# Sixteen places for x, divided mixer steps with a planner margin, and GpSimd's low parts in two instructions

## The chip, the cores and the metric

The kernel runs on one core of one Trainium2 chip. The metric is the device time of one execution in microseconds, taken as the median of several runs. Five engines work in parallel, each through its own list of instructions in order: TensorE (PE; its weight loads are PEld), VectorE (DVE), ScalarE (ACT), GpSimd (POOL) and SyncE (SP), which here issues nearly all transfers from memory.

## What is computed

The input x is 512 positions of 2048 values. Two blocks follow one another. The first has two layers, the second has one layer with two branches side by side:

```python
# first block
for i in range(2):
    h = rmsnorm(x, norm_g[i])
    p = h @ (fox_w_in if i == 0 else swa_w_in)     # q, k, v, gate
    y = fox_attention(...) if i == 0 else swa_attention(...)
    x = x + (y * silu(gate)) @ w_out
x = rmsnorm(x, final_g)
# second block, the mixer
proj = x @ w_in
rw, hg = token_shift(proj[..., :RWKV_COLS]), proj[..., RWKV_COLS:]
o_rwkv = rwkv7_branch(rw, ...)     # 16 heads of 64: S = S*w + (S a) b + v k ; o = S r, group norm
o_hgrn = hgrn2_branch(hg, ...)     # 8 heads of 128: gated linear attention in chunks of 64
y = concat(o_rwkv, o_hgrn) @ w_out
out = layer_norm(ALPHA * x + y)
```

Everything is float32, and the large products are made in three terms so that they keep its accuracy.

## The kernel before

**Tiling.** A weight chunk is a tile `raw` of 128 x 512 (256 KB), loaded by SyncE into one of three buffers. ScalarE copies it in a shorter format into `wh`, GpSimd makes the low part `wl` = `raw` - `wh` in one instruction, and TensorE adds three products for each k-tile of 128: high x high, low x high, high x low (`proj<-hh,wh`, `proj<-hl,wh`, `proj<-hh,wl`). One chunk serves four k-tiles, so twelve matmuls. The activations of a layer are kept in 16 pairs `hh`, `hl`, each made by a *feed* from one k-tile of x (ScalarE makes `hh`, VectorE makes `hl`, and VectorE adds up `rsb` for the norm).

**Order.** `stream` goes over the slots (block of outputs, k-tile) of all weight products and writes them into TensorE's list. Everything else, called side work, is cut into steps that stand in threads: attention heads, the eight RWKV units (`rwkv_unit`, u = 0 to 7, two heads each), the HGRN units. Between two slots `side` takes the steps that are ready. What is ready is decided when the program is built, by a planner: `Clock` keeps a time for each engine, `Engine.cost` gives each instruction's cost, and `ready` compares a step's inputs with TensorE's planned time. `MARGIN` adds 0.1 us to each result and `BUDGET` lets 1.8 us of side work in at a time:

```python
    def ready(self, th):
        return th["steps"] and th["ready"] <= self.clk and all(
            self.ev.get(e, 1e9) <= self.clk for e in th["steps"][0][1]) and self.banks(
                th["steps"][0][0]) <= self.clk
```

A step's instructions on all engines enter the lists together. An engine that comes to one whose input isn't there stands still, with all that is behind it in its list.

**The start.** `start` loads the first tiles of x and the first chunks; eight places for x are in use (tags `t`, `pt`, `yf`, `sg`, two each), and x tile n + 8 is loaded after feed n. The SyncE queue is in order, so chunks behind such a load wait too.

**An RWKV unit.** Its prepare steps (p_kk, p_dec, p_ops and others) make decays and operands, `lev` steps invert a triangular matrix for each of the four chunks of the sequence (VectorE's `invt`, `ly`, `x`; TensorE's small products `t<-td,yh`, `t<-wd,ly`, `t<-ly,wd` of 16 to 32 rows), `ch_z`, `ch_u`, `ch_s` and `ch_o` run the state through the chunks (`chz`, `chu`, `sbd`, `y`), and f_1, f_2, f_3 make the group norm on `zo` with the small sums `gn`; f_3 lets TensorE transpose `zo`. All instructions are recorded by one helper, so every row of the profile has line L182 (L184 after the change).

Of the kernel before, what the change touches and what calls it, by code (L numbers as in the profile page):

```python
# [17 lines left out]
KT = 16  # L18
# [91 lines left out]
class Engine:  # L110
# [15 lines left out]
    def cost(self, m, out, ins, k):  # L126
# [80 lines left out]

class Kern:
    NRAW, NW, LEAD, LEAD_RAW, BUDGET, MARGIN, POOL_LO = 3, 3, 2, 2, 1.8, 0.1, True
# [60 lines left out]
    def split_to(self, end):  # L270
        nc = self.nc
        while self.n_split < min(end, len(self.chunks)):
# [14 lines left out]
            eng = nc.vector if self.n_split in self.extra else nc.gpsimd  # L287
            eng.tensor_tensor(out=lo, in0=t, in1=hi.bitcast(F32), op=ALU.subtract)
# [61 lines left out]
    def ready(self, th):  # L350
        return th["steps"] and th["ready"] <= self.clk and all(
# [3 lines left out]
    def banks(self, f):  # L355

        name = [n for n in f.__qualname__.split(".") if n not in ("<locals>", "f")][-1]
        t = 0.0
        for i, p in enumerate(BANKS.get(name, "")):
# [226 lines left out]
    def start(self):  # L586
# [21 lines left out]
        self.on_slot = on_slot  # L608
        self.load_raw(1)
        load_x(0)  # L610
        self.par = const("par")
        load_x(1)
# [6 lines left out]
        load_x(2)  # L619
        load_x(3)  # L620
        self.load_raw(3)
        for n in range(4, 8):
            load_x(n)
        self.split_to(1)
        feed(0)
        feed(1)
        self.split_to(2)
        feed(2)
        feed(3)

# [671 lines left out]
    def rwkv_unit(self, st, u):  # L1302
# [58 lines left out]
        def p_kk2():  # L1361
# [4 lines left out]
            self.rsqrt(m, rn)  # L1366

        def p_kk3():
            m, rn = S["m"][:, 0:512], S["rn"][:, 0:512]
            self.newton_rsqrt(rn, m, S["sq"])  # L1370
            nc.gpsimd.tensor_tensor(out=S["kq"], in0=S["kq"], in1=rn, op=ALU.mult)

        def p_dec():
# [4 lines left out]
            S["em"] = em = P("em", (128, 2, 4), bufs=3)  # L1378
            nc.scalar.activation(em[:, 0, :], cs[:, :, 64], AF.Exp, scale=-KAPPA)
            mid = P("mid", (128, 4))  # L1380
# [5 lines left out]
        def p_dec2():  # L1386
            cs = S["cs"]
            S["P"], S["Pi"] = P("pr", (128, 4, 129)), P("pt", (128, 4, 128))
# [18 lines left out]
        def p_ops4():  # L1407
            k, r = st["k", u], st["r", u]
            nc.vector.scalar_tensor_tensor(out=r, in0=r, scalar=c2["rk"], in1=k, op0=ALU.mult,
                                           op1=ALU.mult)  # L1410
            S["rh"] = P("pq", dt=F32R)
            nc.scalar.activation(S["rh"], r, AF.Copy)
# [281 lines left out]
        def f_1():  # L1694
# [6 lines left out]
            nc.scalar.activation(S["zo"][:, :, 0, :], of, AF.Square)  # L1701
# [18 lines left out]
        def seq(*items):  # L1720
            r = []
            for f, need, ev, *back in items:
# [12 lines left out]
                   (p_kk2, (), None),  # L1735
                   (p_kk3, (), None),
                   (p_dec, (), None),
# [38 lines left out]
        B = seq((p_ops4, [("mar", u)], "ops"),  # L1776
# [50 lines left out]
    def hgrn_unit(self, st, u):  # L1827
# [17 lines left out]
        def prep2():  # L1845
# [6 lines left out]

            nc.scalar.activation(t2, ls, AF.Abs, bias=c2["bma"])
# [13 lines left out]
        def prep4():  # L1867
# [6 lines left out]
                                    op=ALU.subtract)  # L1874
            nc.scalar.activation(S["d"], S["d"], AF.Exp)
# [167 lines left out]
        def seq(*items):  # L2043
            r = []
            for f, need, ev, *back in items:
# [7 lines left out]
                 (prep2, (), None),  # L2053
                 (prep3, (), None),
                 (prep4, (), None))
# [321 lines left out]
```

## Time and profile before

| | |
|---|---|
| median of three runs | 2966.38 us (2964.68 to 2971.58) |
| profiled execution | 2970.38 us, span 2968.6 us |
| mean granted clock of TensorE | 0.988 of full speed |
| TensorE, VectorE, ScalarE, GpSimd busy | 98%, 51%, 42%, 45% of the span |
| weight chunks split on GpSimd | 847 |

The stages follow in time: fox layer to about 1060 us, window layer to about 1710, RWKV to about 2400, HGRN to about 2800, then the last projection and the layer norm. A busy time counts an instruction's execution; idle time of TensorE is what the waits list explains, and a granted clock below 1 means that TensorE worked at its lower level (1.2 GHz instead of 2.4) for part of the stretch.

### The profile page before, as it was taken

Reading aid. Unit: us, or ns where it says so; the run is one execution under the profiler, and the core shown is the slowest. Engines: PE = TensorE matmul, PEld = TensorE weight load, DVE = VectorE, ACT = ScalarE, POOL = GpSimd, SP = SyncE. Lnnn points to the kernel's source line nnn. Section 1 sums busy time; section 2 is a strip of 40 time slices with the busy share of each in tenths; the row PEclk is TensorE's granted clock in tenths of the full one; section 3 lists DMA queues with packets and bytes.
Section 4 is the critical chain, followed back from the end, with each engine's and each line's share of the span. In section 5 each row is a group of like instructions: output and inputs, shape, how many; then the busy total and the mean of one; then the engine's idle time right before and its main releaser. Section 6 shows DMA issues by size and latency. Waiting matters only on the chain.

```text
span 2968.6 us, 47847 instructions
## 1 busy us (share of the span) xinstructions
PE 2911.0 (98%) x18032; PEld 2351.3 (79%) x18032; DVE 1519.0 (51%) x3374; ACT 1257.6 (42%) x2464; POOL 1332.5 (45%) x1093
## 2 busy tenths in 40 slices
PE   8999999999999999999999999999999999999997
PEld 5888888888888888888888887777777778877786
DVE  6434334343432135555541167777877566666536
ACT  6444444444433344444443354343433345445334
POOL 3444444444436544444446654333333254444583
PEclk9999999999999999999999999999999899999998
DMA  4322232332324432222234423222222222222333
GB/s 141 108 89 91 91 93 93 92 94 88 92 89 160 150 95 77 80 77 78 80 103 150 131 91 90 59 74 70 67 63 75 67 70 72 83 76 77 99 121 121
DMA packets 192087, 275.79 MB, mean 93 GB/s; under 512 B 50576, under 2 KB 65872, under 8 KB 191856
## 3 DMA queue, kind: packets, MB, share of 16 engines
q1 hardware_dynamic: 191856, 272.73, 30.4%
q8 instruction: 142, 2.33, 0.3%
q14 instruction: 89, 0.73, 0.1%
HBM read 254.51 MB, written 18.16 MB: 92 GB/s over the span
## 4 chain that ended last, share of the span: by engine, by line
PE 89%; DVE 5%; issue 2%; POOL 1%; ACT 1%; DMA 0%; SPq 0%; ACTq 0%; POOLq 0%; DVEq 0%
PE proj L182 73%; PE t L182 7%; PE s L182 6%; PE y L182 3%; DVE invt L182 1%; POOL wl L182 1%; DVE hh L182 1%; DVE gn L182 1%; DVE ly L182 1%; DVE zo L182 0%; DMA raw<-in_w_mixo_dram 0%; DVE hn L182 0%; DVE ek L182 0%; DVE raw L182 0%; DVE ez L182 0%
## 5 line engine op out<-in xcount | busy, mean ns | idle before, releaser
L182 POOL TENSOR_TENSOR wl<-raw,wh 128x512 fp32r<-128x512 f32 x847 | 1124.0, 1329 | 1567.3 <-ACT wh L182 1510.1
L182 PE MATMUL proj<-hh,wh 128*128 128x512 f32 x2624 | 1070.1, 408 | 10.8 <-ACT hh L182 6.4
L182 PE MATMUL proj<-hh,wl 128*128 128x512 f32 x2624 | 1034.2, 394 | 3.5 <-POOL wl L182 3.4
L182 PE MATMUL proj<-hl,wh 128*128 128x512 f32 x2624 | 1033.1, 394 | 3.3 <-DVE hl L182 3.1
L182 ACT ACTIVATE wh<-raw 128x512 fp32r<-128x512 f32 x848 | 531.3, 628 | 819.4 <-PE proj L182 588.5
L182 PEld LDWEIGHTS proj<-hh,wh 128*128 128x128 f32 x2624 | 497.2, 189 | 117.1 <-ACT hh L182 7.1
L182 PEld LDWEIGHTS proj<-hh,wl 128*128 128x128 f32 x2624 | 497.1, 189 | 114.9 <-POOL wl L182 7.0
L182 PEld LDWEIGHTS proj<-hl,wh 128*128 128x128 f32 x2624 | 498.4, 190 | 96.0 <-DVE hl L182 6.5
L182 PE MATMUL proj<-yh,wh 128*128 128x512 f32 (+1 forms) x632 | 246.9, 391 | 0.0
L182 PE MATMUL proj<-yh,wl 128*128 128x512 f32 (+1 forms) x632 | 245.6, 389 | 0.3
L182 ACT ACTIVATE t<-t,sm 128x257 f32<-128x257 f32 (+5 forms) x256 | 133.1, 521 | 265.6 <-DVE sm L182 203.7
L182 PE MATMUL proj<-yl,wh 128*128 128x512 f32 (+1 forms) x640 | 242.3, 387 | 0.0
L182 PEld LDWEIGHTS proj<-yh,wl 128*128 128x128 f32 x632 | 118.6, 188 | 26.1 <-POOL wl L182 1.6
L182 PEld LDWEIGHTS proj<-yl,wh 128*128 128x128 f32 x640 | 119.9, 188 | 23.8 <-issue 0.2
L182 PEld LDWEIGHTS proj<-yh,wh 128*128 128x128 f32 x632 | 118.7, 188 | 24.4 <-issue 0.6
L182 DVE TENSOR_TENSOR pt<-proj,t 128x512 f32<-128x512 f32 x32 | 22.1, 691 | 226.3 <-PE proj L182 221.7
L182 DVE TENSOR_SCALAR t<-t,sm 128x256 f32<-128x256 f32 (+3 forms) x256 | 113.5, 475 | 5.6
L182 DVE TENSOR_TENSOR qf<-proj,rsb 128x512 f32<-128x512 f32 x48 | 33.1, 691 | 161.8 <-PE proj L182 161.5
L182 DVE COPY pt<-t 128x384 f32<-128x384 f32 (+1 forms) x80 | 48.5, 607 | 81.6 <-PE t L182 81.6
L182 DVE CUSTOM_DVE_ANT_0 t<-s,c 128x128 f32<-128x128 f32 (+2 forms) x128 | 47.1, 387 | 80.1 <-PE s L182 77.8
L182 PEld LDWEIGHTS t<-ident,t 128*128 128x128 f32 x544 | 69.0, 140 | 21.0
L182 PE MATMUL t<-ident,t 128*128 128x128 f32 x544 | 85.2, 272 | 0.0
(410 smaller groups left out, 3592.4 us busy)
## 6 DMA issues: line engine op xcount, KB each, us to landing
raw<-in_w_mix_dram SPq DMA_DIRECT2D x260, 256.0 KB, 3.0
raw<-in_w_fox_dram SPq DMA_DIRECT2D x256, 256.0 KB, 3.0
raw<-in_w_swa_dram SPq DMA_DIRECT2D x144, 256.0 KB, 3.0
raw<-in_w_foxo_dram SPq DMA_DIRECT2D x64, 256.0 KB, 3.1
raw<-in_w_swao_dram SPq DMA_DIRECT2D x64, 256.0 KB, 3.1
raw<-in_w_mixo_dram SPq DMA_DIRECT2D x64, 256.0 KB, 3.2
c<-cd SPq DMA_DIRECT2D x32, 256.0 KB, 3.7
xd<-pt SPq DMA_DIRECT2D x32, 256.0 KB, 2.4
```

What stands on the lines that cost most here:

```text
L182: r = f(*a, **k)
```

## The change

Four things change. `start` gives each of the 16 tiles of x a place of its own, loads them in an order fixed at the start (par, chunks and groups of x in turn), and feeds run one further ahead. `split_to` makes `wl` on GpSimd in two instructions of 128 x 256. The planner gets other costs (GpSimd's elementwise; 0.25 us more for VectorE operations with two wide inputs and deep, short patterns), a slack for three kinds of steps, and a limit `BACKLOG`: a thread that isn't urgent waits while VectorE's or ScalarE's planned time is over 4 us ahead of TensorE's. And steps that ended in a hand-over to another engine are divided there: p_kk2, p_kk3, p_dec, p_ops4, f_1, and prep2 and prep4 of HGRN; p_kk3 and f_1 stand for them in the diff.

```diff
--- before.py
+++ after.py
@@ -145,11 +145,13 @@
-            return 0.075 + n / (1920.0 if one else 960.0) + 0.06 * bool(points) + 2 * acc
+
+            deep = 0.25 * (len(wide) > 1 and len(out.ap) > 3 and out.ap[-1][1] < 16)
+            return 0.075 + n / (1920.0 if one else 960.0) + 0.06 * bool(points) + 2 * acc + deep
...
-            return max(0.1, 0.00264 * n - 0.11)
+            return max(0.1, 0.00254 * n - 0.05)
...
+SLACK = dict(f_3=1.5, fin3=1.5, ch_z=0.4)
...
-    NRAW, NW, LEAD, LEAD_RAW, BUDGET, MARGIN, POOL_LO = 3, 3, 2, 2, 1.8, 0.1, True
+    NRAW, NW, LEAD, LEAD_RAW, BUDGET, MARGIN = 3, 3, 2, 2, 1.8, 0.1
+
+    BACKLOG = 4.0
...
             nc.scalar.activation(hi, t, AF.Copy)
-            eng = nc.vector if self.n_split in self.extra else nc.gpsimd
-            eng.tensor_tensor(out=lo, in0=t, in1=hi.bitcast(F32), op=ALU.subtract)
+
+            eng, parts = (nc.vector, 1) if self.n_split in self.extra else (nc.gpsimd, 2)
+            for i in range(parts):
+                c = slice(512 // parts * i, 512 // parts * (i + 1))
+                eng.tensor_tensor(out=lo[:, c], in0=t[:, c], in1=hi[:, c].bitcast(F32),
+                                  op=ALU.subtract)
...
     def ready(self, th):
-        return th["steps"] and th["ready"] <= self.clk and all(
+        late = 0.0 if th["first"] else max(
+            self.clock.t["vector"], self.clock.t["scalar"]) - self.BACKLOG
+        f = th["steps"][0][0] if th["steps"] else None
+        return f and max(th["ready"] + SLACK.get(step_name(f), 0.0), late) <= self.clk and all(
             self.ev.get(e, 1e9) <= self.clk for e in th["steps"][0][1]) and self.banks(
                 th["steps"][0][0]) <= self.clk
...
-        def load_x(n):
-            tag, b = (("t", 3), ("pt", 4), ("yf", 2), ("sg", 2))[n % 4]
-            xs.append(self.tmp(tag, bufs=b))
-            nc.sync.dma_start(xs[n], I["x"][n])
+        place = [(t, b) for t, b in (("t", 3), ("pt", 4), ("yf", 2), ("sg", 2), ("vf", 1), ("qf", 1),
+                                     ("vt", 2), ("q0", 1), ("q1", 1)) for _ in range(b)]
+
+        def load_x(end):
+            while len(xs) < end:
+                tag, b = place[len(xs)]
+                xs.append(self.tmp(tag, bufs=b))
+                nc.sync.dma_start(xs[-1], I["x"][len(xs) - 1])
 
         def feed(n):
             self.feed_hi(n, xs[n], self.par, 0)
             self.feed_lo(n, xs[n], self.par, 0, nc.vector)
-            if n < KT - 8:
-                load_x(n + 8)
             self.fed += 1
...
-            while self.fed < min(KT, i // 3 + 4):
+            while self.fed < min(KT, i // 3 + 5):
                 feed(self.fed)
...
         def p_kk3():
             m, rn = S["m"][:, 0:512], S["rn"][:, 0:512]
             self.newton_rsqrt(rn, m, S["sq"])
+
+        def p_kk3b():
+            rn = S["rn"][:, 0:512]
             nc.gpsimd.tensor_tensor(out=S["kq"], in0=S["kq"], in1=rn, op=ALU.mult)
...
             nc.vector.tensor_tensor(out=v8(of), in0=v8(of), in1=bc(g[:, 0, :]), op=ALU.subtract)
-            nc.scalar.activation(S["zo"][:, :, 0, :], of, AF.Square)
+
+        def f_1b():
+            nc.scalar.activation(S["zo"][:, :, 0, :], S["zo"][:, :, 1, :], AF.Square)
...
-        M += seq((f_1, (), "rf1"), (f_2, (), None), (f_3, [("rz", u), ("bonus", u)], ["rfin", "rf3"]))
+        M += seq((f_1, (), "rf1"), (f_1b, (), None), (f_2, (), None), (f_3, [("rz", u), ("bonus", u)], ["rfin", "rf3"]))
```

The order in which instructions stand is the same in both attention layers, but for one transpose in each window unit. It differs at the start and from about 1720 us on.

SyncE's queue at the start, before; `t`, `pt`, `yf`, `sg` are places for tiles of x, and `raw` are chunks of weights:

```order
L182 DMA t<-in_x_dram 128x512
L182 DMA pt<-in_x_dram 128x512
L182 DMA yf<-in_x_dram 128x512
L182 DMA sg<-in_x_dram 128x512
L182 DMA t<-in_x_dram 128x512
L182 DMA pt<-in_x_dram 128x512
L182 DMA yf<-in_x_dram 128x512
L182 DMA sg<-in_x_dram 128x512
L182 DMA raw<-in_w_fox_dram 128x512
L182 DMA t<-in_x_dram 128x512
L182 DMA raw<-in_w_fox_dram 128x512
L182 DMA pt<-in_x_dram 128x512
```

and with the change:

```order
L184 DMA raw<-in_w_fox_dram 128x512
L184 DMA t<-in_x_dram 128x512
L184 DMA pt<-in_x_dram 128x512
L184 DMA raw<-in_w_fox_dram 128x512
L184 DMA pt<-in_x_dram 128x512 x3
L184 DMA yf<-in_x_dram 128x512
L184 DMA raw<-in_w_fox_dram 128x512
L184 DMA yf<-in_x_dram 128x512
L184 DMA sg<-in_x_dram 128x512 x2
L184 DMA vf<-in_x_dram 128x512
L184 DMA raw<-in_w_fox_dram 128x512
L184 DMA qf<-in_x_dram 128x512
```

The loads of x now stand together between the chunks, with nothing that they wait for; before, those from the second group on stand behind the feed that frees their place.

ScalarE in RWKV unit 6 at the group norm's step f_1, before; `zo<-zo` is the Square on VectorE's result, `pm` belongs to a prepare step:

```order
L182 ACTIVATE wh<-raw 128x512 x2
L182 ACTIVATE zo<-zo 128x4x128
L182 ACTIVATE pm<-ek 128x512
L182 ACTIVATE pm<-pm 128x512
L164 ACT_TABLE_LOAD
L182 ACTIVATE pm<-pm 128x512
L182 ACTIVATE wh<-raw 128x512 x3
```

and with the change, where `td`, `wd` belong to another unit's inverse:

```order
L184 ACTIVATE pq<-pr 128x512
L184 ACTIVATE wh<-raw 128x512 x3
L184 ACTIVATE pt<-pt 128x512
L184 ACTIVATE wh<-raw 128x512 x2
L184 ACTIVATE hatt<-s 64x4x64
L184 ACTIVATE pt<-pm 128x256 x2
L184 ACTIVATE zo<-zo 128x4x128
L184 ACTIVATE wh<-raw 128x512 x2
L184 ACTIVATE td<-td,rm 128x8x16 x2
L184 ACTIVATE pt<-pt 128x512
L184 ACTIVATE wh<-raw 128x512
L184 ACTIVATE wd<-t 16x8x16 x2
```

The Square stood behind two splits and ahead of a prepare step with a table load and three splits. It now stands in a step of its own, with splits ahead of it and behind it.

VectorE in unit 4 at the last chunk of the chain, before; `chz` and `chu` are the chain's, `invt`, `ly`, `x` the next unit's inverse:

```order
L182 TENSOR_TENSOR invt<-ly 64x30
L182 TENSOR_TENSOR ly<-ly,invt 64x2x3x5
L182 TENSOR_TENSOR invt<-ly 64x24
L182 TENSOR_TENSOR ly<-ly,invt 64x2x2x6
L182 TENSOR_TENSOR invt<-ly 64x14
L182 TENSOR_TENSOR ly<-ly,invt 64x2x7
L182 TENSOR_TENSOR chz<-t,chz 64x128
L182 TENSOR_TENSOR em<-pr,em 128x3
L182 TENSOR_SCALAR ez<-ez,par_483,der 128x512
L182 COPY chu<-t 64x128
```

and with the change:

```order
L184 SCALAR_TENSOR_TENSOR sbd_15613<-t,em,chf 64x64 x2
L184 TENSOR_TENSOR invt<-ly 64x256
L184 TENSOR_REDUCE x_20963<-invt 64x32
L184 TENSOR_TENSOR invt<-ly 64x256
L184 TENSOR_REDUCE x_20963<-invt 64x32
L184 TENSOR_TENSOR invt<-ly,x_20963 64x256
L184 TENSOR_REDUCE ly<-invt 64x4x8
L184 TENSOR_TENSOR invt<-ly,x_20963 64x256
L184 TENSOR_REDUCE ly<-invt 64x4x8
L184 TENSOR_TENSOR chz<-t,zo 128x128
L184 COPY ly<-ly 64x256
L184 COPY chu<-t 64x128
```

Before, fourteen small operations of the inverse stand ahead of the second `chz`, of which the last five pairs or so are shown in part; with the change, four pairs of wide operations stand ahead of the first `chz`.

TensorE at the same place, before, from the product for `chu` to the one that reads the second `chz`:

```order
L182 MATMUL t<-chu,yh_15079 64x64 x2
L182 MATMUL proj<-hh_93,wh 128x512
L182 MATMUL proj<-hl_105,wh 128x512
L182 MATMUL proj<-hh_93,wl 128x512
L182 MATMUL proj<-hh_94,wh 128x512
L182 MATMUL proj<-hl_106,wh 128x512
L182 MATMUL proj<-hh_94,wl 128x512
L182 MATMUL proj<-hh_94,wh 128x512
L182 MATMUL proj<-hl_107,wh 128x512
L182 MATMUL proj<-hh_94,wl 128x512
L182 MATMUL t<-chz,wd 64x64 x2
```

and with the change, the end of the 18 weight products between `t<-sbd,ar`, from which VectorE makes the first `chz`, and the product that reads it:

```order
L184 MATMUL proj<-hl_105,wh 128x512
L184 MATMUL proj<-hh_93,wl 128x512
L184 MATMUL proj<-hh_94,wh 128x512
L184 MATMUL proj<-hl_106,wh 128x512
L184 MATMUL proj<-hh_94,wl 128x512
L184 MATMUL proj<-hh_94,wh 128x512
L184 MATMUL proj<-hl_107,wh 128x512
L184 MATMUL proj<-hh_94,wl 128x512
L184 MATMUL t<-chz,wd 64x64 x2
```

Nine weight products covered the second `chz`; now 18 and four transposes cover the first.

## Rows read from the trace of the kernel before

**Rows 1.** The page, part 1: each engine's busy time, share of the span, instructions.

```profile
...
PE 2911.0 (98%) x18032; PEld 2351.3 (79%) x18032; DVE 1519.0 (51%) x3374; ACT 1257.6 (42%) x2464; POOL 1332.5 (45%) x1093
...
```

**Rows 2.** Windows by stage: busy us (instructions) of each engine, TensorE's granted clock, DMA.

```profile
...
0.00:100.00 100.00, 87.81 (x392) 63.98 (x393) 56.60 (x99) 56.62 (x98) 40.66 (x36) 0.98 0.44 137
...
1560.00:1710.00 150.00, 150.00 (x662) 123.85 (x661) 25.04 (x30) 52.65 (x84) 92.56 (x73) 1.00 0.45 140
...
1840.00:2000.00 160.00, 155.88 (x1386) 118.75 (x1382) 117.13 (x258) 60.63 (x118) 54.67 (x41) 0.96 0.26 70
2000.00:2200.00 200.00, 190.94 (x1749) 146.78 (x1750) 158.28 (x350) 77.52 (x151) 66.70 (x52) 0.97 0.27 71
2200.00:2400.00 200.00, 193.41 (x1789) 147.90 (x1788) 134.19 (x319) 71.19 (x143) 59.40 (x47) 0.93 0.22 62
...
```

**Rows 3.** TensorE's waits, 0 to 100 us: total, times, longest in us.

```profile
...
PE proj L182 <- DVE hl L182: 3.1, 4, 2.4
...
PE proj L182 <- POOL wl L182: 0.9, 2, 0.6
...
```

**Rows 4.** Timeline of the start: VectorE's feed, SyncE's queue. Start, duration, work.

```profile
...
21.68 1.75 DVE L182 SCALAR_TENSOR_TENSOR hl<-yf,par,hh 128x512 fp32r<-128x512 f32 x1
...
23.50 0.33 SPq L182 DMA_DIRECT2D yf<-in_x_dram  x1
...
```

**Rows 5.** Windows of the start, columns as in rows 2.

```profile
...
5.00:15.00 10.00, 8.49 (x18) 5.39 (x19) 7.10 (x9) 7.03 (x12) 4.04 (x3) 1.00 0.94 314
...
20.00:24.00 4.00, 1.58 (x7) 0.96 (x6) 4.00 (x5) 3.70 (x7) 2.58 (x2) 1.00 0.00 0
24.00:30.00 6.00, 5.70 (x18) 4.23 (x18) 3.66 (x6) 2.06 (x4) 1.30 (x1) 0.72 0.67 219
...
```

**Rows 6.** TensorE's waits, 1710 to 2400 us, columns as in rows 3.

```profile
...
PE t L182 <- DVE chz L182: 5.8, 5, 2.6
PE proj L182 <- ACT wh L182: 3.7, 2, 3.4
PE t L182 <- DVE chu L182: 3.3, 3, 1.6
PE proj L182 <- POOL wl L182: 2.5, 4, 1.2
PE t L182 <- DVE zo L182: 2.2, 3, 1.1
...
```

**Rows 7.** Timeline, 2318 to 2332 us: ScalarE and TensorE; idle time before in brackets.

```profile
...
2324.73 0.63 ACT L182 ACTIVATE zo<-zo 128x512 f32<-128x512 f32 x1 [7.85 <-DVE zo L182]
...
2329.05 0.80 PE L182 MATMUL proj<-hh,wh 128*128 128x512 f32 x1 [3.37 <-ACT wh L182]
...
```

**Rows 8.** Timeline, 2161 to 2174 us: TensorE and VectorE.

```profile
...
2171.05 0.41 PE L182 MATMUL t<-chz,wd 64*64 64x64 f32 x4 [2.61 <-DVE chz L182]
...
2171.91 0.59 DVE L182 TENSOR_TENSOR invt<-ly 64x256 f32<-64x256 f32 x1
2172.53 0.41 DVE L182 TENSOR_REDUCE x<-invt 64x32 f32<-64x256 f32 x1
...
```

**Rows 9.** Timeline, 2180 to 2186 us: GpSimd and VectorE.

```profile
...
2181.87 3.79 POOL L182 TENSOR_TENSOR wl<-raw,wh 128x512 fp32r<-128x512 f32 x3 [4.91 <-ACT wh L182]
...
2182.12 3.56 DVE L182 TENSOR_SCALAR gn<-gn 128x8 f32<-128x8 f32 x3
2185.72 0.17 DVE L182 TENSOR_TENSOR gn<-gn 128x8 f32<-128x8 f32 x1
...
```

**Rows 10.** Groups by form on GpSimd: count, busy us, mean ns, idle before.

```profile
...
L182 POOL TENSOR_TENSOR wl<-raw,wh 128x512 fp32r<-128x512 f32 x847 | 1124.0, 1329 | 1567.3 <-ACT wh L182 1510.1 <-PE proj L182 17.8 <-PE t L182 17.8
...
L182 POOL TENSOR_TENSOR tokv<-tokv,hg 128x256 f32<-128x256 f32 x8 | 6.0, 745 | 0.2 <-PE s L182 0.2
...
```

**Rows 11.** Windows of two stretches with a low clock, columns as in rows 2.

```profile
...
2326.00:2333.00 7.00, 3.81 (x11) 2.72 (x12) 3.64 (x16) 4.02 (x6) 3.74 (x3) 0.76 0.29 61
2343.00:2368.00 25.00, 25.00 (x283) 18.53 (x280) 7.94 (x23) 5.47 (x12) 7.01 (x9) 0.59 0.14 44
...
```

More of the change, by code (lines that the diff above doesn't have):

```diff
@@ L205, with step_name @@
      "ch_u2", "ch_u3", "ch_s", "f_3", "tok", "state", "fin3"), "t"))
+SLACK = dict(f_3=1.5, fin3=1.5, ch_z=0.4)
+def step_name(f):
+    return [n for n in f.__qualname__.split(".") if n not in ("<locals>", "f")][-1]
 class Kern:
-    NRAW, NW, LEAD, LEAD_RAW, BUDGET, MARGIN, POOL_LO = 3, 3, 2, 2, 1.8, 0.1, True
+    NRAW, NW, LEAD, LEAD_RAW, BUDGET, MARGIN = 3, 3, 2, 2, 1.8, 0.1
+    BACKLOG = 4.0
     def __init__(self, tc, I, out):
@@ L355, in banks @@
     def banks(self, f):
-        name = [n for n in f.__qualname__.split(".") if n not in ("<locals>", "f")][-1]
         t = 0.0
-        for i, p in enumerate(BANKS.get(name, "")):
+        for i, p in enumerate(BANKS.get(step_name(f), "")):
             pool, bufs = self.psum[p]
@@ L608, in start @@
         self.on_slot = on_slot
+        self.par = const("par")
         self.load_raw(1)
-        load_x(0)
-        self.par = const("par")
-        load_x(1)
+        load_x(2)
         self.ones = self.tile(self.cp, (128, 128), F32, "ones")
@@ L618, in start @@
         self.load_raw(2)
-        load_x(2)
-        load_x(3)
+        load_x(4)
         self.load_raw(3)
-        for n in range(4, 8):
-            load_x(n)
+        load_x(8)
         self.split_to(1)
@@ L626, in start @@
         feed(1)
+        self.load_raw(4)
+        load_x(12)
         self.split_to(2)
@@ L629, in start @@
         feed(3)
+        self.load_raw(5)
+        load_x(KT)
         def loads():
@@ L1365, in p_kk2, with p_kk2b @@
             nc.vector.tensor_scalar(m, p, 1e-24, None, ALU.max)
-            self.rsqrt(m, rn)
+        def p_kk2b():
+            self.rsqrt(S["m"][:, 0:512], S["rn"][:, 0:512])
         def p_kk3():
@@ L1387, in p_dec2 @@
             cs = S["cs"]
+            S["em"] = em = P("em", (128, 2, 4), bufs=3)
+            nc.scalar.activation(em[:, 0, :], S["mid"], AF.Exp, scale=-KAPPA)
             S["P"], S["Pi"] = P("pr", (128, 4, 129)), P("pt", (128, 4, 128))
@@ L1735, in rwkv_unit @@
                    (p_kk2, (), None),
+                   (p_kk2b, (), None),
                    (p_kk3, (), None),
+                   (p_kk3b, (), None),
                    (p_dec, (), None),
@@ L1772, in rwkv_unit @@
             M += seq((ch_o(c), pre("rf1") if c == 0 else (), ("ch", u, c), 2 if c < 3 else 1))
-        M += seq((f_1, (), "rf1"), (f_2, (), None), (f_3, [("rz", u), ("bonus", u)], ["rfin", "rf3"]))
+        M += seq((f_1, (), "rf1"), (f_1b, (), None), (f_2, (), None), (f_3, [("rz", u), ("bonus", u)], ["rfin", "rf3"]))
         K = seq((p_tok("b"), [("pops", u)] + pre("chs"), None),
                 (p_tok("k"), (), "tok"))
-        B = seq((p_ops4, [("mar", u)], "ops"),
+        B = seq((p_ops4, [("mar", u)], None),
+                (p_ops4b, (), "ops"),
                 (p_ops5, (), None),
@@ L1851, in prep2, with prep2b @@
             nc.vector.tensor_tensor(out=t, in0=ls, in1=f, op=ALU.subtract)
+        def prep2b():
+            ls, t, t2 = S["ls"], S["t"], S["t2"]
             nc.scalar.activation(t2, ls, AF.Abs, bias=c2["bma"])
@@ L1874, in prep4, with prep4b @@
                                     op=ALU.subtract)
+        def prep4b():
             nc.scalar.activation(S["d"], S["d"], AF.Exp)
@@ L2053, in hgrn_unit @@
                  (prep2, (), None),
+                 (prep2b, (), None),
                  (prep3, (), None),
-                 (prep4, (), None))
+                 (prep4, (), None),
+                 (prep4b, (), None))
         if u == 0:
```

7 lines of the change are left out of this document (3 added, 4 removed).

## The prediction

> **What bounds the kernel now.** The page comes first: the matmul row of TensorE stands at 2911.0 us, 98% of the span [rows 1]. So no other engine's busy time matters by itself. A gain can come from two places only: the moments in which TensorE stands still, and the moments in which its clock is low. The windows by stage show where these lie [rows 2]. In 1560 to 1710 us TensorE is busy for 150.00 of 150.00 us at clock 1.00, beside a GpSimd that is busy for 92.56; nothing can be won there. The first 100 us lack 12.2 us, and the three stretches from 1840 to 2400 us, where the RWKV units run, lack 4.1, 9.1 and 6.6 us and have clocks of 0.96, 0.97 and 0.93. A clock of 0.93 over 200 us is 14.0 us of work that a full clock would not have needed; the three together are 6.4 + 6.0 + 14.0 = 26.4 us.
>
> Next, what TensorE waits for. At the start it waits 3.1 us for `hl`, longest 2.4, and 0.9 for `wl` [rows 3]. The timeline there [rows 4] has VectorE on `hl<-yf` from 21.68 to 23.43 us, and SyncE's next x load issued at 23.50 us, right after it: the loads stand behind the feeds. The windows show the price [rows 5]: the DMA engines move nothing in 20 to 24 us, where TensorE is busy for 1.58 of 4.00, and in the 6 us behind it the clock is 0.72. The row ahead, 5 to 15 us, has 314 GB/s at a share of 0.94: what the queues can move.
>
> In 1710 to 2400 us [rows 6] five rows make 17.5 us: `chz` 5.8, ACT's `wh` 3.7, `chu` 3.3, GpSimd's `wl` 2.5, `zo` 2.2. Two places show the mechanism. At 2324.73 us ScalarE starts a Square on `zo` after 7.85 us of idleness for VectorE's `zo`; the splits of weights queue behind it, and TensorE stops for 3.37 us until `wh` comes at 2329.05 [rows 7]. At 2171.05 TensorE gets `chz` 2.61 us late [rows 8]: VectorE, in order, had 14 small inverse operations to do first.
>
> Third, the lock between VectorE and GpSimd [rows 9]. Three `gn` operations of VectorE take 3.56 us beside three GpSimd subtractions that take 3.79; the next one alone takes 0.17. One VectorE operation passes for each GpSimd instruction.
>
> **The start.** Sixteen places for x instead of eight in flight: no load waits for a feed, and the feeds run one ahead. The bytes stay. 16 tiles of x and the 12 chunks used beside them are 7.3 MB, which at 314 GB/s [rows 5] take 23 us; TensorE's matmuls come every 150 / 662 = 0.227 us in the densest stage [rows 2], and 48 slots of three take 33 us. So the loads keep ahead. The 2.4 us for `hl` go, the clock's 6 us x 0.28 = 1.7 us go with them, and the 0.9 for `wl` (below): **-5.0 us**. Bounds: 0 if VectorE stays as late as it is, -7 if the idle time before the first product shrinks too. At about 97 us 18 products move behind side work; they only change places.
>
> **Two halves of `wl`.** Today 1329 ns for 512 columns, x847; the nearest row for 256 columns is 745 ns [rows 10]. Two halves would take 1.49 against 1.33 us, 0.16 us more per chunk, or nothing if the difference in that row is the lock's. In the densest stage [rows 2] 73 instructions x 0.16 = 12 us would bring GpSimd to 104 of 150: cover remains, so 0. TensorE waits once more for each chunk; it waits there already now, and has 150.00 of 150.00 [rows 2], so a wait that is fulfilled is worth 0 too. Without that cover the extra would be 0.16 us for each chunk near the edge. The gain: the first half serves two of the chunk's four k-tiles and is ready 0.66 us earlier. Four waits of 2.5 in all, longest 1.2 [rows 6], shrink by up to 0.66 each: 2.0 us at most go. I take **-2.0**; bounds 0 and -2.5.
>
> **Divided steps.** The Square of `zo` becomes a step of its own, begun only when the planner sees its input done. Both `wh` waits (3.7) stand behind such a Square. In the order after, the Square of unit 6 has five splits ahead of it since `pq<-pr`, and the vector steps are let run ahead first. **-3.7**; bounds 0 and -3.7. The same holds for the other divided steps (p_kk2, p_kk3, p_dec, p_ops4, prep2, prep4), which no wait of TensorE's list names: 0 each, covered by the products around them, and at worst they move their step later by one round of the planner, some 1.8 us of `BUDGET`, off the path.
>
> **Planner margin.** The output's transposes now wait for 1.5 us of slack: `zo`'s 2.2 us go to about 0.2, **-2.0**. `chz` and `chu` together have 9.1 us. How much of this goes I take from the one place that I followed. In unit 4 the order after puts eight operations of the last inverse level ahead of `chz<-t,zo`, four pairs of 0.59 + 0.41 and gaps [rows 8], about 4.2 us, plus `chz` 0.29 and one or two half locks of 0.6: 5.1 to 5.7. TensorE's cover there is 18 products x 0.227 plus four transposes, 4.5 us. The stall of 2.6 becomes 0.6 to 1.2: a share of 0.46 stays at the upper end. 9.1 x 0.54 = **-4.9**; bounds 0 (they only move) and -9.1. Longer planned costs and the backlog limit hold steps back elsewhere, and whatever is held must come out later: I add **+1.0** for new waits, between 0 and the size of one of today's longest, 3.4.
>
> **The clock.** Of the 26.4 us, three falls stand behind waits, like 2326 to 2333 us [rows 11]: 7 us x 0.24 = 1.7 each, 5.0 in all. As one of the three waits may stay long enough, I count two and a half: **-4.2**. The other 21.4 us lie at steps of small products (16 to 32 rows, the units' 16-row inverse level) where TensorE is never idle: the largest, 2343 to 2368 us, has 25.00 of 25.00 busy at 0.59, 10.25 us lost [rows 11]. The change gives TensorE the same small products there, in five of eight units again with only three weight products between the two groups. I leave the 21.4 us in. The Trainium skill, "TensorE: Matmul & The Clock Gate", Part 1, says that the clock falls to 1.2 GHz when the engine is idle and returns to 2.4 GHz when it is busy. By that rule alone the falls would go with the waits, and the sum would be 21 us lower; the row with 25.00 of 25.00 busy speaks against it.
>
> **The sum.** -5.0 - 2.0 - 3.7 - 2.0 - 4.9 + 1.0 - 4.2 = -20.8 us against the profiled execution's 2970.4 (span 2968.6 and 1.8 around it): 2949.6. That execution lay 4.0 above the median of the three timed runs, 2966.4, so the median after is about 2945.6, said as **2946**. Its own range is 2938 to 2957, mostly by how much of `chz` and `chu` stays. A difference of 0.2%, 6 us, is about what a measurement of this kernel can tell from no change.
>
> **Rivals.** *The waits only move:* a planner that counts other costs makes another order from 1720 us on, with other close calls; only the start stays, 2966.4 - 5.0 = 2961. For it: the 18-product place above is already 0.6 us short. Against: longer costs and slack all point to later reading of results, and no engine but TensorE is over 80% busy in any stage from 1840 on. 0.15.
> *Everything goes:* the remaining 4.9 us of the five wait rows, the 1.0, and the 21.4 + 0.8 us of the clock: 2946 - 28 = 2918. For it: five small-product steps fell and others of the same kind didn't, so it isn't the products alone. Against: TensorE is busy throughout those. 0.10. The Clock Gate page's rule would end here.
> *The change does nothing for waits:* the lock passes from the first half straight to the second, VectorE is held just as long, and TensorE's waits return at once: 2966. Against: the three rows of the lock show one VectorE operation let through for each GpSimd instruction, back to back. 0.06.
> *Slower:* the denser order brings the small-product steps next to one another with less work between them, and all eight get a piece like that of 2343 us: 8 x 10.25 = 82 against 21.4, which is +60.6 - 20.8: 3006. It decides from three more such pieces on (31 us against 20.8 + 6). For it: the piece at 2343 came behind a TensorE that had waited 3.37 us just ahead; against: only one of the five was that long. 0.09.
>
> **How the numbers follow.** The likeliest case has 0.60. The range leaves out *everything goes* and *slower*, 0.19, and takes in the rest and the bounds. Downward these are -4.2 (all of `chz` and `chu`), -2.0 (the start), -0.5 (`wl`), -1.0 (no new waits) and half of the small-product falls, -10.7: 2946 - 18 = 2928, and I set 2926. Upward it ends at 2964, where only the 2.4 us of `hl` are won. Faster by over 0.2%: 0.58 + 0.10 + half of the moved waits, 0.08 = 0.76; within: 0.02 + 0.07 + 0.06 = 0.15; slower 0.09.
>
> **What the profile after would show.** Start: DMA never at 0.00 ahead of 30 us, no `hl` wait over 1 us, clock over 0.9 in 24 to 30. Halves: `wl` rows of 128x256, x1694, at 0.6 to 0.75 us, and `gn` operations under 1 us. Steps: no `wh` wait in 1710 to 2400 of over 1 us. Margin: `chz` and `chu` at about 4 us, `zo` under 0.5. Clock: low stretches only at small products, 15 to 25 us lost. The prediction is wrong if the halves cost over 0.8 us each in 1560 to 1710 and TensorE waits for GpSimd there, if waits under new names exceed 5 us, or if the clock's loss leaves 15 to 25.

## The result, and the profile after

The changed kernel takes **2935.18 us** in the median of four runs (2933.35 to 2943.02), against 2966.38. The ratio is 0.9897, with an interval of 0.9875 to 0.9919: 31 us less, between 24 and 37. The forecast was 2946, with a range of 2926 to 2964. The profiled execution took 2943.02 us (span 2941.2), 27.4 less than that of before and 7.8 above the median of its own kernel.

The page of the kernel after, part 1, columns as in [rows 1]:

```profile
...
PE 2902.6 (99%) x18032; PEld 2350.7 (80%) x18032; DVE 1478.4 (50%) x3374; ACT 1261.7 (43%) x2464; POOL 1523.2 (52%) x1940
...
```

GpSimd has 191 us more to do, VectorE 41 us less, with the same number of VectorE instructions. The windows of the kernel after, by stage, against [rows 2]:

```profile
...
0.00:100.00 100.00, 93.38 (x459) 70.91 (x461) 64.03 (x117) 60.48 (x108) 57.06 (x69) 1.00 0.46 148
...
1560.00:1710.00 150.00, 150.00 (x661) 123.83 (x660) 26.86 (x31) 52.57 (x83) 99.01 (x128) 1.00 0.43 136
...
1840.00:2000.00 160.00, 158.51 (x1353) 121.02 (x1352) 112.36 (x257) 62.55 (x119) 65.98 (x76) 0.96 0.28 73
2000.00:2200.00 200.00, 198.06 (x1729) 152.44 (x1728) 148.82 (x336) 75.47 (x145) 84.26 (x98) 0.95 0.28 74
2200.00:2400.00 200.00, 196.81 (x1878) 151.63 (x1875) 145.73 (x352) 85.96 (x167) 74.98 (x95) 0.99 0.24 67
...
```

TensorE's idle time in the first 100 us fell from 12.2 to 6.6 us, and in the three RWKV stretches from 19.8 to 6.6 us. The clock's loss there went only from 26.4 to 6.4 + 10.0 + 2.0 = 18.4 us, and the stretch ahead of them, 1710 to 1840 us, lost 5 us more than before. At 1560 to 1710 us nothing could be won, and nothing was lost: GpSimd went from 92.56 to 99.01.

Where the gain lies in time is seen by counting the weight products (`proj`): the 300th starts 9.6 us earlier after its kernel's beginning than before, the 6500th 10.0, the 7500th 13.2, the 8500th 24.2, the last 27.6. So 10 us come from the start, none from the attention layers, and 18 from the mixer.

The windows of the start, against [rows 5], and TensorE's waits in the first 100 us, against [rows 3]:

```profile
...
5.00:15.00 10.00, 8.38 (x22) 5.78 (x23) 8.56 (x10) 9.86 (x18) 6.63 (x7) 1.00 0.98 362
20.00:24.00 4.00, 4.00 (x20) 3.30 (x19) 3.17 (x5) 4.00 (x8) 2.57 (x3) 1.00 0.30 85
24.00:30.00 6.00, 6.00 (x28) 4.99 (x27) 6.00 (x6) 5.49 (x11) 6.00 (x6) 1.00 0.37 109
...
```

```profile
...
PE proj L184 <- ACT hh L184: 6.2, 1, 6.2
PE proj L184 <- DVE hl L184: 0.4, 1, 0.4
```

The hole of 20 to 24 us is gone, with the low clock behind it. The row of 5 to 15 us now moves 362 GB/s, so the 314 of [rows 5], which the prediction took for what the queues can move, was not their limit. TensorE's waits of 1710 to 2400 us, against [rows 6], first the four small rows of the list before that [rows 6] leaves out:

```profile
...
PE t L182 <- DVE ly L182: 0.9, 2, 0.7
PE y L182 <- DVE chu L182: 0.8, 3, 0.4
PE t L182 <- DVE sbd L182: 0.3, 1, 0.3
PE t L182 <- ACT zo L182: 0.2, 1, 0.2
```

and the whole list after:

```profile
...
PE proj L184 <- DVE raw L184: 2.3, 2, 1.8
PE t L184 <- DVE zo L184: 1.7, 1, 1.7
PE t L184 <- ACT zo L184: 1.0, 2, 0.5
PE y L184 <- DVE chu L184: 0.6, 1, 0.6
PE s L184 <- DVE tokv L184: 0.5, 1, 0.5
PE t L184 <- DVE pt L184: 0.5, 1, 0.5
PE t L184 <- DVE ly L184: 0.4, 1, 0.4
PE t L184 <- DVE chz L184: 0.3, 1, 0.3
```

The list went from 19.7 to 7.3 us: `wh` and `wl` are no longer in it, `chz` fell from 5.8 to 0.3, `chu` from 3.3 and 0.8 to 0.6, `zo` stayed (2.2 and 0.2 before, 1.7 and 1.0 after), and `raw`, the evacuation of a finished weight product, is new.

The lock, against [rows 9]; VectorE's and GpSimd's timeline of the kernel after at 2040 us:

```profile
...
2040.17 0.87 DVE L184 SCALAR_TENSOR_TENSOR gn<-gn 128x8 f32<-128x8 f32 x2
2041.07 0.67 DVE L184 TENSOR_TENSOR gn<-gn 128x8 f32<-128x8 f32 x1
2041.77 0.86 DVE L184 SCALAR_TENSOR_TENSOR gn<-gn 128x8 f32<-128x8 f32 x2
2042.67 0.65 DVE L184 TENSOR_TENSOR gn<-gn 128x8 f32<-128x8 f32 x1
...
```

```profile
...
2040.28 1.44 POOL L184 TENSOR_TENSOR wl<-raw,wh 128x256 fp32r<-128x256 f32 x2 [1.82 <-ACT wh L184]
2041.87 1.42 POOL L184 TENSOR_TENSOR wl<-raw,wh 128x256 fp32r<-128x256 f32 x2 [0.16 <-ACT wh L184]
```

A small operation that meets a half now takes about 0.66 us, where three that met whole ones took 3.56, 1.19 each. (In each row marked x2 the first of the two operations started ahead of the half and took 0.17 us.) The Trainium skill, "SBUF — State Buffer", "Who interferes with whom", calls the port that the two engines share an exclusive lock: the engine that comes second is blocked fully, not slowed down. These rows agree: while halves follow one another without a gap, one VectorE operation gets through for each of them.

The lock was also at work in the place of [rows 8], where the prediction saw only VectorE's order. Of the 14 small operations ahead of the late `chz`, eleven took 0.17 or 0.18 us each. The other three took 3.77 us together, beside three GpSimd instructions, of which only the last splits weights. VectorE's rows, then GpSimd's, in the kernel before:

```profile
...
2164.85 1.29 DVE L182 TENSOR_TENSOR invt<-ly 64x24 f32<-64x24 f32 x1
...
2166.38 1.19 DVE L182 TENSOR_TENSOR invt<-ly 64x30 f32<-64x30 f32 x1
2167.60 1.29 DVE L182 TENSOR_TENSOR ly<-ly,invt 64x30 f32<-64x30 f32 x1
...
```

```profile
...
2164.80 1.30 POOL L182 TENSOR_TENSOR bk<-pq,ez 128x512 f32<-128x512 f32 x1 [1.21 <-PE t L182]
2166.18 1.34 POOL L182 TENSOR_TENSOR bk<-bk,pt 128x512 f32<-128x512 f32 x1
2167.57 1.28 POOL L182 TENSOR_TENSOR wl<-raw,wh 128x512 fp32r<-128x512 f32 x1
```

At 0.17 us each the three would have taken 3.3 us less (an estimate), more than the 2.61 us that TensorE waited.

### The profile page after: what moved, and what is told of

Same layout as the page of the kernel before. It is cut to its first block, busy times and chain, and to the rows that moved or that the text cites. A ratio compares the mean times of both kernels' runs of the same rounds, so it can differ in the third digit from the quotient of the medians.

```text
span 2941.2 us, 49366 instructions
## 1 busy us (share of the span) xinstructions
PE 2902.6 (99%) x18032; PEld 2350.7 (80%) x18032; DVE 1478.4 (50%) x3374; ACT 1261.7 (43%) x2464; POOL 1523.2 (52%) x1940
## 4 chain that ended last, share of the span: by engine, by line
PE 95%; DVE 3%; ACT 1%; DMA 1%; POOL 1%; issue 0%; SPq 0%; ACTq 0%; DVEq 0%; POOLq 0%
PE proj L184 78%; PE t L184 8%; PE s L184 6%; PE y L184 3%; DVE hh L184 1%; DMA raw<-in_w_mixo_dram 0%; DVE gn L184 0%; DVE hn L184 0%; DVE ez L184 0%; POOL wl L184 0%; DVE raw L184 0%; ACT hh L184 0%; DMA up<-in_w_up_dram 0%; POOL bk L184 0%; DVE yl L184 0%
## 5 line engine op out<-in xcount | busy, mean ns | idle before, releaser
L184 POOL TENSOR_TENSOR wl<-raw,wh 128x256 fp32r<-128x256 f32 x1694 | 1316.0, 799 | 1368.8 <-ACT wh L184 1322.1
L184 PEld LDWEIGHTS proj<-yl,wh 128*128 128x128 f32 x640 | 119.9, 188 | 24.2 <-issue 0.2
L184 DVE TENSOR_SCALAR t<-t,sm 128x256 f32<-128x256 f32 (+3 forms) x256 | 104.5, 440 | 5.6
```

What stands on the lines that cost most here:

```text
L184: r = f(*a, **k)
```

## The experiments

Each ratio is to the kernel before, run on the same chip, with its 95% interval in brackets; 0.001 is 3 us. The intervals reach 3 to 5 us to each side, so differences between two of these kernels that are under some 6 us are not told apart.

**The parts alone.** The first kernel puts the new `start` into the kernel before. Its core:

```diff
-            if n < KT - 8:
-                load_x(n + 8)
...
-            while self.fed < min(KT, i // 3 + 4):
+            while self.fed < min(KT, i // 3 + 5):
...
+        load_x(8)
...
+        load_x(KT)
```

> The kernel before with the new start alone (sixteen places for x, fixed load order, feeds one ahead); the order from 130 us on is that of before. The prediction's term says -5.0 us: 2961. Rival, read from the profile after: its 300th and its 5000th weight product both start 9.8 to 9.9 us earlier than before, so the start is worth twice the term: 2956. Second rival: later steps give some of it back, since VectorE's and GpSimd's phases shift against TensorE's: 2963 to 2966.

Measured: 0.9978 (0.9967 to 0.9989), 6.5 us. Its 300th weight product starts 7.5 us earlier than before. The term, 5.0, was a little small; the 10 us read from the kernel after are too much for the start alone. The other 2 come with the halves: with both, in before's order (the sixth kernel), the 300th product starts 8.7 us earlier.

The second has the halves in the order of before; the planner counts one instruction:

```diff
-            eng = nc.vector if self.n_split in self.extra else nc.gpsimd
-            eng.tensor_tensor(out=lo, in0=t, in1=hi.bitcast(F32), op=ALU.subtract)
+            eng, parts, noted = (nc.vector, 1, 1) if self.n_split in self.extra else (nc.gpsimd, 2, 1)
+            for i in range(parts):
+                c = slice(512 // parts * i, 512 // parts * (i + 1))
+                eng.eng.tensor_tensor(out=lo[:, c], in0=t[:, c], in1=hi[:, c].bitcast(F32),
+                                      op=ALU.subtract)
...
+                self.clock.note(eng.name, eng.cost("tensor_tensor", lo[:, c], ins, {}), [lo[:, c]], ins,
...
```

> The kernel before with only the low parts in two instructions; the planner still counts one whole instruction, so every other engine's order is that of before. Theory: halves are worth the prediction's -2.0 for wl and some of chz and chu through shorter locks, together -2 to -5: 2961 to 2964. Rival A: the halves are the main cause of the mixer's gain (VectorE freed sooner): about -18, 2948. Rival B: halves do nothing (more GpSimd time, 799 ns each): 2966.

Measured: 0.9958 (0.9943 to 0.9973), 12.5 us: between the theory and its first rival, and six times the prediction's term. A group of VectorE operations in 1710 to 2400 us, in the kernel before and in this one, and then this kernel's group on GpSimd:

```profile
...
L182 DVE TENSOR_TENSOR invt<-ly,x 64x256 f32<-64x256 f32 x16 | 15.6, 972 | 0.6
...
```

```profile
...
L182 DVE TENSOR_TENSOR invt<-ly,x 64x256 f32<-64x256 f32 x16 | 11.0, 690 | 0.6
...
```

```profile
...
L290 POOL TENSOR_TENSOR wl<-raw,wh 128x256 fp32r<-128x256 f32 x1694 | 1310.4, 796 | 1368.8 <-ACT wh L182 1334.2 <-PE t L182 12.3 <-PE s L182 8.1
...
```

The halves cost GpSimd 1.59 instead of 1.33 us a chunk and give VectorE back 40 us over the whole execution (1519.0 to 1479.2 us busy), in the same order. At the place of [rows 8], where two of the three GpSimd instructions are no splits, `chz` still comes 2.53 us late.

The third is the kernel after with whole parts in after's order (one instruction is made, two are counted):

> The kernel after with the low part in one instruction again; the planner counts as for two, so every other engine's order is that of after. Theory: +2 to +5 on 2935: 2937 to 2940, with small wl waits back. Rival A (halves are the main cause): +18, 2953. Rival B (halves do nothing): 2935.

Measured: 0.9980 (0.9968 to 0.9992): 24 us slower than after, so the theory's +2 to +5 fell and Rival A came nearest, though it too was short by 6. Its `invt<-ly,x` takes 993 ns.

The fourth is the kernel after with the old `start`:

> The kernel after with the start of before; its order from 130 us on is that of after. If start and mixer add up, the difference to after is that of the new start on the kernel before: by the term +5 (2940), by the positions of the weight products +10 (2945). If the start's gain in after needs the halves (VectorE's feeds were locked behind whole subtractions), this kernel keeps part of it: 2940 to 2942, and the new start alone on before gives less than 10.

Measured: 0.9923 (0.9909 to 0.9938). The start is worth 6 to 8 us on the kernel after, held against its two measurements (0.9902 below), as on the one before; the 300th weight product comes 6.5 us later than in after.

**Do they add up?** The fifth counts whole parts as whole ones, so the planner makes an order for them:

> The kernel after with the low part in one instruction, and the planner counts one whole instruction too, so it makes its own order. The run with whole parts in the order made for halves lost nearly everything (ratio 0.998). Theory 1: most of that loss is that the halves themselves free VectorE (its invt<-ly,x operations go from 0.70 to 0.99 us with whole parts); then a planner that knows of whole parts recovers little: 2958 to 2963, ratio 0.997 to 0.999. Theory 2: the loss came from an order that counted on halves it did not have; then it recovers most: 2942 to 2950, ratio 0.992 to 0.994.

Measured: 0.9944 (0.9930 to 0.9959), between the two, just past the slow end of theory 2: about half of the 24 us lost by the third kernel came from an order that counted on halves, and about half, 13 us, is what the halves are worth, as on the kernel before. Against the start alone it shows what planner and divided steps bring without halves: 0.0034, 10 us.

The sixth has start and halves in before's order:

> The kernel before with the new start and the halves, in before's order of the mixer; what is left to after is the planner's numbers and the divided steps. If parts add up: -6.7 (start alone) -12.5 (halves alone) = -19, 2949, ratio 0.9935, and planner and divided steps are worth another 10 us in after. Rival: halves and start overlap (both cure the same waits of the first 130 us, 4 us of the halves' gain), 2952 to 2953. Second rival: all of after's gain is start and halves, 2937.

Measured: 0.9937 (0.9924 to 0.9949), 18.7 us against 19 for the parts: they add up. TensorE's waits in 1710 to 2400 us still have the long rows of before:

```profile
...
PE t L182 <- DVE chz L182: 6.4, 6, 2.5
PE proj L182 <- ACT wh L182: 3.2, 2, 2.9
...
```

**Smaller parts.** The seventh makes four instructions for each chunk, in after's order:

```diff
-            eng, parts = (nc.vector, 1) if self.n_split in self.extra else (nc.gpsimd, 2)
+            eng, parts, noted = (nc.vector, 1, 1) if self.n_split in self.extra else (nc.gpsimd, 4, 2)
```

> The kernel after with the low part in four instructions of 128x128, every other engine's order as in after. If what counts is how long one GpSimd instruction keeps a VectorE operation out: VectorE's locked operations get shorter again (invt<-ly,x from 0.70 towards 0.64), another 2 to 5 us come off: 2930 to 2933, ratio 0.988. If the fixed cost of an instruction wins: a half took 0.75 to 0.80 us against 0.67 for half of a whole one, so quarters may take 0.42 to 0.5 each, 1.7 to 2.0 us per chunk where a chunk's twelve products take 2.7; GpSimd's own late results make TensorE wait: 2938 to 2950. No change (2935): both small.

Measured: 0.9955 (0.9941 to 0.9969), 17 us slower than after. GpSimd's group and TensorE's waits of the first 100 us:

```profile
...
L302 POOL TENSOR_TENSOR wl<-raw,wh 128x128 fp32r<-128x128 f32 x3388 | 1651.3, 520 | 1051.5 <-ACT wh L184 1004.4 <-PE t L184 21.0 <-PE proj L184 15.9
...
```

```profile
...
PE t L184 <- DVE vf L184: 3.5, 1, 3.5
```

GpSimd's timeline at the start, and the first of TensorE's waits behind 2400 us:

```profile
...
17.40 22.88 POOL L302 TENSOR_TENSOR wl<-raw,wh 128x128 fp32r<-128x128 f32 x34
...
```

```profile
...
PE t L184 <- POOL pm L184: 2.9, 1, 2.9
...
```

Four quarters take 2.08 us, two halves 1.60, a whole one 1.33. VectorE's work fell by another 59 us, to 1419.8, but GpSimd, at 63% of the span, was late where its own results count. At the start it works for 22.88 us without a pause, ScalarE waits 4.0 us for a place for `wl`, and `vf` starts at 50.29 us instead of 46.38; with this wait, and a fall of the clock right behind it, 6.6 us of after's gain at the start are gone. From about 2470 us on another 8 us go; there `pm`, an operation of GpSimd's own, stands behind eight quarters, and TensorE waits 2.9 us for it.

**The clock.** The eighth cuts the steps of small products in two (`lev16`, and `lev16b` likewise):

```diff
-                 (lev16, (), None),
-                 (lev16b, (), None),
+                 (lev16, (), None), *[(lev16_cut(q), (), None) for q in CUT[1:]],
+                 (lev16b, (), None), *[(lev16b_cut(q), (), None) for q in CUT[1:]],
```

> The kernel after with the two steps of small products (16-row level of the inverse, lev16 and lev16b) cut in two each, so that weight products of 128 columns stand between the halves. All falls of the clock in after's mixer (25.5 us lost) lie at these steps, with TensorE busy. If it is the density of small products that the clock answers to, the loss falls to 5 to 15 us and the time by 10 to 20: 2917 to 2927, ratio 0.983 to 0.986. If it answers to waits only, nothing moves: 2935. If the longer chain of steps makes the units late: 2940 to 2950.

Measured: 0.9918 (0.9901 to 0.9934). Its profiled execution lost 18.8 us to the clock in the mixer and waited 2.7 us in 1710 to 2400 us, both less than after; its median is no better. One profile can't settle it, since the next kernel shows how far this loss moves by itself.

The ninth is the kernel after again:

> The kernel after itself, on the same chip as the three that take parts from it: 2931 to 2938, ratio 0.988 to 0.991. Its ratio is the one that the three are held against, and that of the kernel with the small products cut in two (0.9918) too.

Measured: 0.9902 (0.9887 to 0.9918), 2941.35 us against 2968.02 on that chip. That is 29 us for the whole change, measured a second time. The instructions are those of after; its profiled span is 2948.0. The windows around two units' small products in this run, and then in the first profile of the kernel after:

```profile
...
1960.00:2000.00 40.00, 39.92 (x375) 29.67 (x375) 22.54 (x48) 15.68 (x31) 9.38 (x12) 0.70 0.21 55
2040.00:2075.00 35.00, 33.86 (x346) 25.31 (x345) 22.11 (x48) 13.59 (x28) 8.11 (x11) 0.76 0.21 62
...
```

```profile
...
1960.00:2000.00 40.00, 40.00 (x421) 29.99 (x420) 24.84 (x56) 19.19 (x37) 9.44 (x12) 0.83 0.24 62
2040.00:2075.00 35.00, 33.18 (x398) 25.04 (x397) 22.20 (x54) 15.63 (x34) 9.69 (x12) 0.90 0.14 45
...
```

One program, busy TensorE in both, and the clock at 0.70 or 0.83, 0.76 or 0.90: over the mixer this is 10 us of lost clock between two executions, whose spans differ by 6.8.

Every recorded execution has a granted clock, so the time lost to it can be estimated for each: the span times 1 minus the clock. Some 9 us of it lie behind the last product in every kernel and cost nothing, and the clock's three digits leave 1.5 us open.

| kernel | executions | lost to the clock: mean (lowest to highest), us | the rest of the time, us |
|---|---|---|---|
| before, on three chips | 45 | 35 (27 to 51) | 2933 |
| after, both measurements | 9 | 30 (21 to 44) | 2910 |
| first: start alone | 12 | 32 (27 to 39) | 2930 |
| second: halves alone | 6 | 28 (21 to 36) | 2927 |
| third: whole parts in after's order | 11 | 43 (38 to 50) | 2919 |
| fourth: after with the old start | 6 | 31 (21 to 35) | 2913 |
| fifth: whole parts in their own order | 6 | 33 (29 to 38) | 2917 |
| sixth: start and halves in before's order | 6 | 27 (21 to 29) | 2921 |
| seventh: quarters | 6 | 38 (32 to 41) | 2916 |
| eighth: small products cut | 6 | 35 (26 to 44) | 2908 |
| tenth: joined steps | 4 | 73 (66 to 75) | 2924 |
| eleventh: no slack | 6 | 40 (32 to 44) | 2913 |
| twelfth: no backlog limit | 4 | 34 (29 to 38) | 2908 |

The rest varies by 1 to 3 us (one standard deviation) between executions of a kernel; what makes one program's times differ is mostly the clock. Of the change, 24 us are in the rest and 5, give or take 5, in the clock. And for the eighth kernel the six executions answer more than the profile did: the loss did not fall by the 10 to 20 us of the first theory. Cutting these steps in two did not keep the clock up.

**Planner and divided steps.** The tenth joins the divided steps again, all but p_dec:

```diff
-                   (p_kk2, (), None),
-                   (p_kk2b, (), None),
-                   (p_kk3, (), None),
-                   (p_kk3b, (), None),
+                   (joined(p_kk2, p_kk2b), (), None),
+                   (joined(p_kk3, p_kk3b), (), None),
...
-        M += seq((f_1, (), "rf1"), (f_1b, (), None), (f_2, (), None), (f_3, [("rz", u), ("bonus", u)], ["rfin", "rf3"]))
+        M += seq((joined(f_1, f_1b), (), "rf1"), (f_2, (), None), (f_3, [("rz", u), ("bonus", u)], ["rfin", "rf3"]))
```

> The kernel after with its divided steps joined again (p_kk2, p_kk3, p_ops4, f_1, prep2, prep4); the planner's numbers, halves and start stay. The prediction gave the division 3.7 us, all for the Square of zo and the splits behind it: 2938 to 2940, with ACT's wh waits of 3 us back in the RWKV stage. Rival: the planner's slack and backlog limit hold such steps back anyway, so the division is worth nothing (2935). Second rival: the divided steps carry the whole 10 us that is left beside start and halves: 2945.

Measured: 1.0090 (1.0075 to 1.0105): 56 us slower than after and 27 slower than the kernel before. No theory had this. TensorE's waits of 1710 to 2400 us:

```profile
...
PE proj L184 <- DVE raw L184: 14.8, 6, 3.2
PE t L184 <- DVE zo L184: 8.2, 4, 4.4
PE proj L184 <- DVE esz L184: 3.0, 1, 3.0
...
```

The timeline of VectorE and then of TensorE at one of the six places:

```profile
...
2057.49 0.69 DVE L184 TENSOR_TENSOR zo<-zo,gn 128x512 f32<-128x512 f32 x1
...
2058.99 0.75 DVE L184 SCALAR_TENSOR_TENSOR yl<-t,par,yl 128x512 f32<-128x512 f32 x1
2059.78 0.75 DVE L184 SCALAR_TENSOR_TENSOR yl<-yl,par,esz 128x512 f32<-128x512 f32 x1
2060.45 0.68 DVE L184 TENSOR_TENSOR raw<-proj,rsb 128x512 f32<-128x512 f32 x1
...
```

```profile
...
2058.33 0.63 PE L184 MATMUL t<-ident,zo 128*128 128x128 f32 x4 [0.28 <-DVE zo L184]
2061.28 0.47 PE L184 MATMUL proj<-hh,wh 128*128 128x512 f32 x1 [2.32 <-DVE raw L184]
...
```

The evacuation of a unit's z block (`raw<-proj`) needs the event `rfin` of the unit two before, which f_3 sets. Where f_3 hasn't come by then, the program forces it in: transposes of `zo`, two operations on `yl`, the evacuation, and only then is a bank free for TensorE's next product. With joined steps the group norm comes so late that nearly every unit pays this. That the slack and the backlog limit, made for divided steps, are what delays it is argued from the code, not shown: the kernel before has joined steps and no such wait. The clock goes down with the waits: 64.7 us lost in the mixer, summed over windows of 5 us, against 25.5 and 35.9 in the two profiles of after. By the table this is the larger part of the 56 us: some 14 are in the rest. No wait for `wh` is back, though the Square is joined to its step again.

The eleventh takes out the slack:

```diff
-SLACK = dict(f_3=1.5, fin3=1.5, ch_z=0.4)
+SLACK = {}
```

> The kernel after without the slack for f_3, fin3 and ch_z. The prediction gave zo 2.0 us for it; the profile after has 2.7 us of zo waits in spite of it, and chz at 0.3. If slack is what holds these down: zo and chz waits of 6 to 9 us, 2939 to 2942. If not: 2935, waits as in after.

Measured: 0.9944 (0.9930 to 0.9957), 12 us slower than the ninth kernel. `zo` waits rise to 4.7 us in 1710 to 2400, `ly`, `sbd`, `pt` and `chz` to 5.7 together, in all 12.7 against 3.9 in the ninth kernel's list. By its ratio the slack is worth as much as all that planner and divided steps bring beside start and halves. By the table only some 4 us of this lie in the rest; the other part is the clock's, and not clear of its spread.

The twelfth takes out the backlog limit:

```diff
-    BACKLOG = 4.0
+    BACKLOG = 1e9
```

> The kernel after without the backlog limit: steps of threads that aren't urgent are let in however far VectorE and ScalarE are planned ahead of TensorE. If VectorE's queue in order is what made chz, chu and wh late, the limit carries the larger part of the planner's 10 us: 2940 to 2945, with chz and chu waits of 5 us and more back. Rival: the limit seldom binds (VectorE is busy for three quarters of the RWKV stage at most), 2935.

Measured: 0.9904 (0.9889 to 0.9919), the same as after. A single `wh` wait of 2.8 us is back, behind ScalarE's part of an evacuation (`ez<-er`) and not behind a Square, and no other wait of over 1.1 us in all; the rival holds.

## Why the prediction was right, point by point

**The start** (-5.0): right; 6.5 alone, 6 to 8 in the kernel after. It priced `hl`, `wl` and the clock; `vf` and `wh`, 0.8 to 0.9 each, went as well.

**Two halves** (-2.0): the term of the sum that was mis-sized. It measured 12.5 us on the kernel before and about 13 on after's planner. The step that failed is "The gain: the first half serves two of the chunk's four k-tiles": it priced only TensorE's own waits for `wl`, four of them, and that price was about right (2.5 to 0.9 us). The lock rows stood in the same text, but what they are worth for all of VectorE's operations was never summed, and the clock's share was put at nothing. VectorE lost 40 us of its work to whole parts: 19 in the RWKV units, where the largest group, the inverse's `invt<-ly,x`, has 4.5, and 19 in the HGRN units and behind them. In the profile of halves alone the waits of 1710 to 2400 us went only from 19.7 to 16.2 us (`chu` 3.3 to 0.8, `wl` 2.5 to 0.9), 4 us came at the start, and the clock lost 12 us less. The table tells the halves' share of the last from this execution's chance: over all executions the rest fell by 6.5 us and the clock's loss by 7.7, give or take 5. So about half of what the halves bring is standing time and about half is the clock's; by what way they raise the clock is not shown.

The forecast halves, "0.6 to 0.75 us", took 0.80 in the mean and 0.74 in the median: the bound of 0.16 us a chunk became 0.27. GpSimd had the room, as the text had it: in 1560 to 1710 us it got 6.5 us more to do, not 12, and neither list of after shown above names `wl`. With quarters it no longer had it, at the start and behind 2400 us.

**Divided steps, margin, new waits** (-3.7 - 2.0 - 4.9 + 1.0): the sum was right, 10 us measured twice, by the sixth kernel against the ninth and by the fifth against the first. That it was right is luck, since its parts were not and their errors cancel: `chz` and `chu` gave 9 where 4.9 was forecast, `zo` gave nothing where 2.0 was forecast, and new waits (`raw`, `pt`, `tokv`) took 3.3 where 1.0 was. `wh` went, 3.7 as forecast, but that the divided Square did it is not shown: in the tenth kernel, where it is joined again, no `wh` wait is back, and in the twelfth, where it is divided, one is. And dividing steps and planner aren't separate terms: joined steps under the new numbers cost 56 us, not the 3.7 of one Square. That each edit can be priced by the waits that it takes away was wrong for this pair.

**The clock** (-4.2): the mechanism held in part, the size can't be told. The three falls behind waits of before are gone. Of the five falls in the profile after, four stand behind no wait; the fifth begins at 2050.8 us, at the end of a wait of 1.8 us for `raw`, and the ninth kernel's clock fell at the same place ahead of that wait. But the falls at the small products, left at 21.4 us, came out at 25.5 us in one profile of after and 35.9 in the next (5 us windows, mixer alone). Both lie outside the 15 to 25 us that the prediction named, the first by half a microsecond, and by its own sign it was wrong there. Over all executions the clock lost 5 us less, give or take 5: near the 5.9 that the clock had in the forecast with the start's 1.7, and too near nothing to be claimed. The Trainium skill, "TensorE: Matmul & The Clock Gate", Part 1, ties the lower clock to an idle engine. The case *everything goes*, where its rule would end, did not happen, and 40.00 of 40.00 us busy at 0.83 is a second row against idleness as the only cause here.

**The rivals.** *Waits only move* and *nothing for waits* are out: the list fell from 19.7 to 7.3 us. *Slower* is out for this change, though the tenth kernel shows how near it was, by another way than the one forecast: late group norms. The time came out 11 us under the forecast, and the 10.5 us that the halves gave beyond their term are nearly all of that.

## What to carry to other kernels

A GpSimd operation that locks VectorE out costs twice, once on GpSimd and once in the VectorE operations that stand still beside it. Cut it until GpSimd's own lateness shows: here two parts were better than one and than four. A planner's margins, its costs and the cutting of its steps are one setting: an order made for other durations (the third kernel) or other steps (the tenth) gives back most of the gain (24 of 31 us) or more than all of it (56). And before a difference of a few microseconds is put down to an edit, look at what one program differs by itself: here the nine executions of the kernel after lie between 2933 and 2950 us, mostly by the clock.

## What the runs showed of the hardware

GpSimd's subtraction takes 1329, 799 and 520 ns in the mean for 512, 256 and 128 columns in this kernel (before, after and quarters). Those with no VectorE operation beside them take 1289, 737 and 460 ns, which is 2.16 ns a column and a fixed part of about 185 ns. The lock holds GpSimd up too: 61 of the 847 whole parts and 262 of the 1694 halves took over 15% longer than the middle one, up to 2.3 and 2.2 us, and every one of these had a VectorE operation beside it.

The granted clock fell in the same program at different units' small products from one execution to the next, with TensorE busy throughout. Why is open: cutting those steps in two did not lower the loss (35 us against 30), and halves on GpSimd alone, which leave TensorE's order as it was, did (28 against 35).
